# A hybrid decoder trunk on one core: two low parts of w_out by accumulating DMA, four sample readouts in one VectorE step each, the last samples and the last scan step moved up

## The chip, the cores and the metric

The kernel runs on one core of one Trainium2 chip. The metric is the device time of one execution in microseconds (us). A core has TensorE (PE; its weight loads are listed apart as PEld), VectorE (DVE), ScalarE (ACT), GpSimd (POOL) and SyncE (SP), which here only issues DMAs. Each works through its own list of instructions in a fixed order, and semaphores hold an instruction back until what it needs is there.

## What is computed

One step of a decoder layer for 512 new tokens of one prompt and one new token of each of 8 running sequences, 520 columns in all: a half-step SwiGLU FFN, a mixer, a second half-step FFN, a final norm, all in fp32. The mixer, cut to what matters:

```python
proj = h @ w_in                                   # u_pool, z, xbc, dt
pool_out = pooling mixer of u_pool                # 512 columns
xs, B, C = silu(causal_conv(xbc))
y, h_new = ssd_scan(xs, dt, A, B, C, state)       # chunks of 128 tokens, 2 groups of 8 heads
y = (y + d_skip * xs) * silu(z)
y = rms_norm per group (512 columns each) * ssd_norm
out = concatenate([pool_out, y]) @ w_out          # 1536 -> 1024
h = h + out
```

For a sample (one token of a running sequence) the scan is one step: the readout is the state's rows (128 per pair of heads) times C, summed over the 128 state columns, times the decay, plus a term from the new token.

## The kernel before

**Matmuls in three terms.** Every large product is made of fp32r matmuls of a high and a low part: `mm3` (lines 146, 149, 150) issues whi·xhi, whi·xlo and wlo·xhi into one PSUM bank. A weight unit is a tile of 128x1024 (512 KB). `load_unit` fetches it into one of four raw buffers with a DMA on SP's queue (L142); `split` has ScalarE cast it to whi (L134) and VectorE subtract to get wlo = raw - whi (L136). There are three homes for a pair of parts (thi/tlo, and two of whi/wlo), so a unit's cast waits until the matmuls of the unit before last but one are done. The FFNs have a second way, `part_by_dma` (L230): ScalarE makes the high part and then minus the high part, and a DMA of GpSimd's queue adds the weights from HBM to it.

**The mixer's order** is written by hand in three strings. `CONV_PLAN` does the inputs of the convolution and the first scan steps; `GATE_PLAN` the rest; `LAST_PLAN` joins the last units of w_out to the second FFN's start. A letter names a stage: z a unit of the gate's projection, p, c, m the pooling, A and B the two halves of a scan step (`ssd_a`, `ssd_b`; numbers 0 to 7 are four chunks of two groups), s that many samples, G the gate of one group (it needs all samples and scan steps of its group), H its norm, o, g, h the units of w_out for the pooled part and for groups 0 and 1 (`wout`), e small outputs. The order of the plan gives each instruction its rank. A scheduler at compile time then lays out each engine's list: by rank, among what its own model of the time holds ready. So VectorE's list interleaves stages, while TensorE's follows the plan nearly everywhere. Instructions under `keep_in_program_order` (the samples') stand behind all that their engine has from earlier in the plan.

**A sample** (`sample`, L1088): two loads on SP's queue, C's row for all partitions (L1090, two buffers) and the state of four head pairs (L1092, four buffers); VectorE multiplies them, 128x512 (L1094); ScalarE sums each quarter with four activations that accumulate into a column of `ysm` (L1097: an ACTIVATE and a read of the accumulator each).

**A scan step's second half** (`ssd_b`): TensorE makes yo, pst and yd in three PSUM banks; GpSimd scales the state hst (L1214), VectorE adds pst (L1215), combines yo and yd (L1218, L1219) and puts the result into X (L1222). In the mixer the PSUM pool has eight banks, taken in turn; a unit of w_out takes four, which L1243 adds to h.

**Gate and norm.** `gate` (G): scales ysm, adds it into X's sample columns (L1104, L1105, L1257), multiplies X by silu of z (L1254, L1259). `gate_out` (H): squares on ScalarE (L1265), adds on VectorE (L1268), a matmul with ones into psr_y (L195, plain fp32), root (L198) and reciprocal (L199), then the factor (L1276) and high and low part of the group's operand catg (L1277, L1278).

Of the kernel before, what the change touches and what calls it, by code (L numbers as in the profile page):

```python
# [13 lines left out]
ALU = mybir.AluOpType  # L14
# [21 lines left out]
LOW_ON_DVE = ((2, 0), (3, 0), (KF - 1, 1))  # L36
ON_ACT = 4
STATES = ((1, 1, 1, 1), (6, 17, 19, 20, 21), 4)
LOW_BY_DMA = {1: (2, 3, 4, 5, 6), 2: (*range(7), 9, 11)}

CONV_PLAN = (
    "b0 b1 d0 b2 b3 x0 x1 v0 d1 x2 x3 d2 X0 p0 y0 c0 A0 k0 p1 x4 m0 x5 B0 c1 p2 m1 A1 x6 c2 A2 B1 x7 X1 m2 A3"
)
GATE_PLAN = (
    "z0 B2 A4 z1 B3 p3 s1 z2 B4 s2 z3 c3 A5 s2 s2 z4 m3 B5 s2 A6 z5 e0 s2 G0 z6 A7 s2 z7 B6 s2 o0 H0 o1 B7 s1 G1 o2 "
    "o3 g0 g1 H1 g2 g3"
)
LAST_PLAN = "h0 h2 h1 n0 h3 n1 n2 n3"
# [15 lines left out]
def tile_trunk_step(ctx: ExitStack, tc: tile.TileContext, ins: dict, outs: dict):  # L64
# [165 lines left out]
    def part_by_dma(hi, lo, s, home):  # L230
        nc.scalar.copy(hi, s)
        nc.scalar.activation(out=lo, in_=hi.bitcast(F32), func=AF.Copy, scale=-1.0)
        nc.gpsimd.dma_start(out=lo, in_=home, accum_op=ALU.add)
# [22 lines left out]
    class Ffn:  # L256
# [175 lines left out]
        def quarter(self, f):  # L432
# [7 lines left out]
            if len(src.shape) == 3:  # L440
                h, l = (t.rearrange("p (j c) -> p j c", j=4) for t in (hi, lo))
            if f in LOW_BY_DMA[self.i] and (f, 1) not in LOW_ON_DVE:
                part_by_dma(h, l, src, self.dram[f][1][:, 512:])
# [90 lines left out]
        def stream(self, before, last_chunk):  # L534
# [6 lines left out]
            for t in tiles:  # L541
                for _ in range(STATES[0][t.d] if not isinstance(t, int) else t in STATES[1]):
                    next(self.states, None)
# [68 lines left out]
        def down_by_half(self, c, lo, after, wd):  # L612
            n = KF - lo
            banks, units = {}, []
            for d in range(KD):
                if d < STATES[2]:
                    next(self.states)
# [156 lines left out]

    ps[0] = tc.alloc_tile_pool(name="ppm", bufs=8, space=PSUM, reuse_waits="tile")
    mixer(tc, ins, outs, dict(locals()))
    f2["xg"].release()
    xa[0].release()
# [69 lines left out]
def mixer(tc, ins, outs, e):  # L848
    nc = tc.nc
    cst, act, wp, tmp, dr, pool = (e[x] for x in ("cst", "act", "wp", "tmp", "dr", "pool"))  # L850
    ones, queued, squared = e["ones"], e["queued"], tuple(e["added"])
    bank, load_unit, mm3, ws, v, rstd, rstds, vec, h, nx2, raw_tile, open_f2, fin, fill = (
        e[x] for x in ("bank", "load_unit", "mm3", "ws", "v", "rstd", "rstds", "vec", "h", "nx2", "raw_tile",
                       "open_f2", "fin", "fill"))
    xh, xl, _, r = nx2[0]
# [195 lines left out]
    ysm = mp.tile([P, NX, NS], F32, tag="ysm", name="ysm")  # L1051
# [4 lines left out]
    def rows_bc(b, a, g):  # L1056
        return scr_bc.rearrange("b (a g n) -> b a g n", a=2, g=2)[b, a, g].unsqueeze(0).to_broadcast([P, P])
# [27 lines left out]
        nc.vector.tensor_tensor(out=sxdt[:, gs], in0=sdt[:, gs], in1=X[:, gs, SEQ:NT], op=ALU.mult)  # L1085


    def sample(b, g):  # L1088
        cb = tmp.tile([P, HB], F32, tag="ta", name=f"cb{b}{g}")[:, :P]
        nc.sync.dma_start(out=cb, in_=rows_bc(b, 1, g))  # L1090
        h0 = mp.tile([P, 4, P], F32, tag="h0", bufs=4, name=f"h0_{b}{g}")
        nc.sync.dma_start(out=h0, in_=ins["state_ssm"][:, b, 4 * g : 4 * g + 4])  # L1092
        tc.keep_in_program_order(
            nc.vector.tensor_tensor(out=h0, in0=h0, in1=cb.unsqueeze(1).to_broadcast([P, 4, P]), op=ALU.mult))  # L1094
        for q in range(4):
            tc.keep_in_program_order(
                nc.scalar.activation(out=junk, in_=h0[:, q], func=AF.Copy,  # L1097
                                     accum_out=ysm[:, 4 * g + q, b : b + 1]))
# [53 lines left out]
    def ssd_a(c, g):  # L1152
        cs = slice(c * CH, (c + 1) * CH)
        pb = bank(f"pb{c}{g}")
        nc.tensor.transpose(pb[:, :P], BC[:, g, cs], ident)
        nc.tensor.matmul(pb[:, P : 2 * P], BC[:, g, cs], BC[:, 2 + g, cs], start=True, stop=True)
        bt = mp.tile([P, P], F32, tag="bt", bufs=3, name=f"bt{c}{g}")
        nc.scalar.copy(bt, pb[:, :P])
        scm = mp.tile([P, P], F32, tag="scm", bufs=3, name=f"scm{c}{g}")
        nc.vector.tensor_tensor(out=scm, in0=pb[:, P : 2 * P], in1=tri, op=ALU.mult)  # L1160
        px = bank(f"px{c}{g}")
        for q in range(4):
            nc.tensor.transpose(px[:, q * P : (q + 1) * P], X[:, 4 * g + q, cs], ident)
        ab = mp.tile([P, 8, P], F32, tag="ab", bufs=3, name=f"ab{c}{g}")
        nc.sync.dma_start(out=ab, in_=scr_acs[c * NH + 8 * g : c * NH + 8 * g + 8].unsqueeze(0).to_broadcast([P, 8, P]))
        dtc = tok[:, 0, c, 8 * g : 8 * g + 8]
        atc = tok[:, 1, c, 8 * g : 8 * g + 8]
        we = mp.tile([P, 8], F32, tag="we", bufs=2, name=f"we{c}{g}")
        nc.gpsimd.tensor_tensor(out=we, in0=ab[:, :, CH - 1], in1=atc, op=ALU.subtract)
        nc.scalar.activation(out=we, in_=we, func=AF.Exp)  # L1170
        E = cd = None
        if c > 0:
            E = mp.tile([P, 4, P], F32, tag="E", bufs=2, name=f"E{c}{g}")
            for j in range(2):
                nc.scalar.activation(out=E[64 * j : 64 * j + 64], in_=ab[64 * j : 64 * j + 64, j::2, :], func=AF.Exp)
            cd = mp.tile([P, 8], F32, tag="cd", bufs=2, name=f"cd{c}{g}")
            nc.scalar.activation(out=cd, in_=ab[:, :, CH - 1], func=AF.Exp)
        G = ab
        for q in range(ON_ACT):
            nc.scalar.activation(out=G[:, q], in_=ab[:, q], func=AF.Relu, scale=-1.0, bias=atc[:, q : q + 1])  # L1180
        for q in range(ON_ACT, 8):
            nc.vector.tensor_scalar(out=G[:, q], in0=ab[:, q], scalar1=atc[:, q : q + 1], scalar2=0.0,
                                    op0=ALU.subtract, op1=ALU.min)
        with queued(*(held["silu"] if (c, g) == (3, 0) else ())):
            nc.scalar.activation(out=G[:, :ON_ACT], in_=G[:, :ON_ACT], func=AF.Exp, scale=-1.0)
            held["exp"] = nc.scalar.activation(out=G[:, ON_ACT:], in_=G[:, ON_ACT:], func=AF.Exp)
        xdt = mp.tile([P, 8, 64], F32, tag="xdt", bufs=2, name=f"xdt{c}{g}")
        nc.vector.tensor_tensor(out=xdt, in0=px.rearrange("p (a b) -> p a b", a=8),
                                in1=dtc.unsqueeze(2).to_broadcast([P, 8, 64]), op=ALU.mult)
        xw = mp.tile([P, 8, 64], F32, tag="xw", bufs=2, name=f"xw{c}{g}")  # L1190
        nc.gpsimd.tensor_tensor(out=xw, in0=xdt, in1=we.unsqueeze(2).to_broadcast([P, 8, 64]), op=ALU.mult)
        with queued(*(held["catp"] if (c, g) == (0, 0) else ())):
            nc.vector.tensor_tensor(out=G, in0=G, in1=scm.unsqueeze(1).to_broadcast([P, 8, P]), op=ALU.mult)
        pair[c, g] = bt, xdt, xw, G, E, cd
# [35 lines left out]
            nc.vector.tensor_tensor(out=zbox[0][:, j, hs], in0=bs[b][:, :HB], in1=r[:, hs], op=ALU.mult)  # L1230

    def wout(cat, j, d2, fin=None):
        wh, wl = load_unit(ins["w_out"][j, d2], 1024, f"wo{j}{d2}", behind.get((j, d2), ()))
        for d in (2 * d2, 2 * d2 + 1):
            for b, hs in enumerate(HALVES):
                if d != 1 or j != 2:
                    ps = bank(f"wo{j}_{d}{b}")
                else:
                    ps = e["ps"][0].tile([P, 512], F32, tag="A", bufs=2, name=f"wo{j}_{d}{b}")
                for k in range(4):  # L1240
                    i = (d % 2) * 4 + k
                    mm3(ps[:, :HB], ws(wh, i), ws(wl, i), cat[:, 0, k, hs], cat[:, 1, k, hs], k == 0, k == 3)
                nc.vector.tensor_tensor(out=h[:, d, hs], in0=ps[:, :HB], in1=h[:, d, hs], op=ALU.add)  # L1243
                if fin is not None:
                    fin(d, b, hs)

    cats, behind = {}, {}
# [35 lines left out]

    smp = [(b, g) for g in range(2) for b in range(NS)]

    def samples(n):
        for _ in range(n):
            if smp:
                sample(*smp.pop(0))

    pooled, box = [], {}

    def ssd(c):
        return c % NC, c // NC

    def outs_a():
# [14 lines left out]
        "c": lambda j: pooled[j][0](),  # L1311
        "m": lambda j: pooled[j][1](),
        "s": samples,
        "A": lambda j: ssd_a(*ssd(j)),
        "B": lambda j: ssd_b(*ssd(j)),
        "z": zproj,
        "o": lambda j: wout(catp, 0, j),
        "G": gate,
        "H": gate_out,
        "g": lambda j: wout(cats[0], 1, j),  # L1320
        "h": lambda j: wout(cats[1], 2, j, fin),
        "n": fill,
        "e": lambda j: outs_a(),
# [101 lines left out]
```

## Time and profile before

| | |
|---|---|
| Median of 3 runs | 962.92 us (962.7 to 964.66) |
| The profiled execution | 963.72 us, its span 961.9 us |
| Instructions | 19663 |
| HBM read and written | 128.67 MB and 7.34 MB |
| POOL busy | 144.9 us (15%) |

The span runs from the first to the last instruction of the profiled execution. The profile lists busy time of each engine; a wait is put down to the engine, line and tile that came last, as "who <- for whom: total, times, longest"; the chain of waits follows the end of the program back through what released each step. In a row of the timeline the numbers are start and duration in us, and brackets hold the idle time before it and what ended it. In a row of a tile they are shortest, median and longest duration in ns, with the first and last start. A matmul is pipelined, so its duration is longer than its distance to the next.

### The profile page before, as it was taken

The page shows a single profiled execution, that of the slowest core. Times are in us where ns is not written, and L with a number is a line of the kernel's source. Part 1 is how long each engine was busy: PE and PEld are TensorE (multiplying, and loading weights), DVE is VectorE, ACT ScalarE, POOL GpSimd, SP SyncE. Part 2 cuts the span into 40 slices and gives each one's busy share as a digit, 9 for nine tenths or more (in the row PEclk, how much of TensorE's full clock was granted, in tenths as well). Part 3 has the DMA queues.
Part 4 walks back from the last instruction along what each step waited for, and adds up shares of the span by engine and source line. Part 5 has one row for each costly group of instructions (what it writes and reads, how often), then busy time and mean ns, then how long its engine had stood idle before and what let it go on. Part 6 is the DMA issues. An engine that isn't in the chain of part 4 may idle for free. (4 is left out here: it accounts for less than half of the span.)

```text
span 961.9 us, 19663 instructions
## 1 busy us (share of the span) xinstructions
PE 945.5 (98%) x7652; PEld 926.2 (96%) x7652; DVE 852.3 (89%) x1460; ACT 641.2 (67%) x1208; POOL 144.9 (15%) x228
## 2 busy tenths in 40 slices
PE   9999999999999999999999999999999999999996
PEld 8999999999999999999999999999999999999995
DVE  6999899998988788779979998898889999989886
ACT  7777756677566455485688645777776676766763
POOL 0011100001000001046252000112112101122120
PEclk9999999999999999999999999999999999999998
DMA  7665553455544243363355323457666646666642
GB/s 210 181 166 149 142 165 112 123 147 141 159 123 115 87 133 101 93 195 117 111 157 166 108 89 121 110 126 171 166 154 188 160 126 155 174 176 175 185 144 90
DMA packets 53629, 137.29 MB, mean 143 GB/s; under 512 B 7640, under 2 KB 15768, under 8 KB 53536
## 3 DMA queue, kind: packets, MB, share of 16 engines
q1 hardware_dynamic: 39840, 104.18, 33.6%
q0 software_dynamic: 13424, 31.73, 17.2%
q8 instruction: 60, 0.98, 0.4%
q14 instruction: 33, 0.27, 0.1%
q10 hardware_dynamic: 272, 0.13, 0.0%
HBM read 128.67 MB, written 7.34 MB: 141 GB/s over the span
## 5 line engine op out<-in xcount | busy, mean ns | idle before, releaser
L476 ACT COPY ac<-A 128x260 f32<-128x260 f32 x85 | 31.7, 373 | 34.7 <-PE A L150 33.5
L412 DVE TENSOR_TENSOR s<-raw 128x1024 f32<-128x1024 f32 x39 | 47.6, 1220 | 3.6 <-DMA raw<-in_w2gu 2.5
L476 ACT COPY ac<-BE 128x260 f32<-128x260 f32 x41 | 15.4, 376 | 30.0 <-PE BE L150 29.0
L146 PE MATMUL inx<-xh_mx,whi_inx 128*128 128x260 f32 x112 | 31.8, 284 | 0.0
L149 PE MATMUL inx<-xl_mx,whi_inx 128*128 128x260 f32 x112 | 31.6, 282 | 0.0
L150 PE MATMUL inx<-xh_mx,wlo_inx 128*128 128x260 f32 x112 | 31.6, 282 | 0.0
L977 DVE SCALAR_TENSOR_TENSOR A<-U,h,A 128x544 f32<-128x544 f32 x36 | 28.8, 799 | 1.1 <-ACT A L975 0.7
L295 PE MATMUL P<-x,raw 128*128 128x260 f32 x128 | 28.9, 387 | 0.0
L295 PEld LDWEIGHTS P<-x,raw 128*128 128x128 f32 x128 | 24.6, 193 | 4.0 <-DMA raw<-in_w1gu 0.3
L146 PE MATMUL wo<-catg,whi_wo 128*128 128x260 f32 x96 | 27.6, 287 | 0.0
L134 ACT CAST thi<-raw 128x1024 fp32r<-128x1024 f32 (+1 forms) x14 | 14.2, 1012 | 20.0 <-PE wo L149 9.9
L150 PE MATMUL wo<-catg,wlo_wo 128*128 128x260 f32 x96 | 27.2, 283 | 0.0
L149 PE MATMUL wo<-catg,whi_wo 128*128 128x260 f32 x96 | 27.1, 282 | 0.0
L1097 ACT ACTIVATE junk<-h 128x128 f32<-128x128 f32 x64 | 19.7, 308 | 7.9 <-DVE h L1094 6.5
L150 PE MATMUL A<-xth_f,qs 128*128 128x260 f32 x84 | 24.0, 286 | 0.9 <-DMA qs<-in_w2gu 0.8
L1139 ACT ACTIVATE so<-br,sxdt 128x128 f32<-128x128 f32 x64 | 22.5, 375 | 3.3 <-DVE room L1141 3.1
L146 PE MATMUL A<-xth_f,qs 128*128 128x260 f32 x84 | 23.9, 284 | 0.0
L149 PE MATMUL A<-xtl_f,qs 128*128 128x260 f32 x84 | 23.7, 282 | 0.0
L237 DVE TENSOR_TENSOR gs<-gq,gs 128x780 fp32r<-128x780 f32 (+1 forms) x28 | 23.2, 829 | 0.4 <-ACT gs L236 0.4
L146 PE MATMUL inz<-xh_mx,whi_inz 128*128 128x260 f32 x80 | 22.9, 287 | 0.0
L149 PE MATMUL inz<-xl_mx,whi_inz 128*128 128x260 f32 x80 | 22.7, 284 | 0.0
L150 PE MATMUL inz<-xh_mx,wlo_inz 128*128 128x260 f32 x80 | 22.6, 283 | 0.0
(2530 smaller groups left out, 4747.3 us busy)
## 6 DMA issues: line engine op xcount, KB each, us to landing
raw<-in_w2gu SPq DMA_DIRECT2D x44, 512.0 KB, 4.2
raw<-in_w1gu SPq DMA_DIRECT2D x41, 512.0 KB, 4.1
raw<-in_w_in SPq DMA_DIRECT2D x24, 512.0 KB, 3.6
raw<-in_w1d SPq DMA_DIRECT2D x16, 512.0 KB, 4.3
raw<-in_w2d SPq DMA_DIRECT2D x16, 512.0 KB, 4.6
raw<-in_w_out SPq DMA_DIRECT2D x12, 512.0 KB, 3.6
ab<-scr_acs SPq DMA_DIRECT2D x8, 512.0 KB, 4.5
h<-in_state_ssm SPq DMA_DIRECT2D x16, 256.0 KB, 3.5
```

Of the source, the lines that this page charges most:

```text
L134: cast = nc.scalar.copy(h, src)
L146: first = nc.tensor.matmul(ps, whi, xhi, start=start, stop=False, **kw)
L149: nc.tensor.matmul(ps, whi, xlo, start=False, stop=False, **kw)
L150: nc.tensor.matmul(ps, wlo, xhi, start=False, stop=stop, **kw)
L237: low = nc.vector.tensor_tensor(out=lo, in0=s, in1=hi.bitcast(F32), op=ALU.subtract)
L295: mm = nc.tensor.matmul(self.banks[f, u][b][:, :HB], ws(self.raw[f][:, u], j + 4 * q), xg[:, slot[q]], start=j == q == 0, stop=j == 3 and ...
L412: nc.vector.tensor_tensor(out=s1, in0=diag, in1=up0, op=ALU.add)
L476: self.copied = nc.scalar.copy(keep, out[:, :HB]).ins
L977: nc.vector.scalar_tensor_tensor(out=A[:, :n], in0=U[:, j : j + n], scalar=w(j), in1=A[:, :n], op0=ALU.mult, op1=ALU.add)
L1097: nc.scalar.activation(out=junk, in_=h0[:, q], func=AF.Copy, accum_out=ysm[:, 4 * g + q, b : b + 1]))
L1139: nc.scalar.activation(out=o[:, q], in_=br, func=AF.Copy, scale=sxdt[:, j, b : b + 1]))
```

## The change

Three edits, all in the mixer's second half.

- `wout` takes the low part of units (1,0) and (1,1), which are g0 and g1, by `part_by_dma`.
- `sample` gets a flag: then VectorE sums all four quarters with one `tensor_reduce` of 128x4x128 into 128x4 instead of ScalarE's four activations. The letter r in the plan sets it.
- In `GATE_PLAN`, s1 and s2 at the front become r2 and r2; the last s1 goes, so each later sample comes one place sooner; B7 moves from behind o1 to in front of it.

```diff
+OUT_LOW_BY_DMA = ((1, 0), (1, 1))
...
 GATE_PLAN = (
-    "z0 B2 A4 z1 B3 p3 s1 z2 B4 s2 z3 c3 A5 s2 s2 z4 m3 B5 s2 A6 z5 e0 s2 G0 z6 A7 s2 z7 B6 s2 o0 H0 o1 B7 s1 G1 o2 "
+    "z0 B2 A4 z1 B3 p3 r2 z2 B4 r2 z3 c3 A5 s2 s2 z4 m3 B5 s2 A6 z5 e0 s2 G0 z6 A7 s2 z7 B6 s2 o0 H0 B7 o1 G1 o2 "
     "o3 g0 g1 H1 g2 g3"
 )
...
-    def sample(b, g):
+    def sample(b, g, reduce):
...
+        if reduce:
+            tc.keep_in_program_order(
+                nc.vector.tensor_reduce(out=ysm[:, 4 * g : 4 * g + 4, b], in_=h0, axis=mybir.AxisListType.X, op=ALU.add))
+            return
         for q in range(4):
...
     def wout(cat, j, d2, fin=None):
-        wh, wl = load_unit(ins["w_out"][j, d2], 1024, f"wo{j}{d2}", behind.get((j, d2), ()))
+        src, name = ins["w_out"][j, d2], f"wo{j}{d2}"
+        if (j, d2) in OUT_LOW_BY_DMA:
+            raw = raw_tile(name)
+            nc.sync.dma_start(out=raw, in_=src)
+            wh, wl = e["weight_homes"](1024, name, wp, 3, ("whi", "wlo"))
+            e["part_by_dma"](wh, wl, raw, src)
+        else:
+            wh, wl = load_unit(src, 1024, name, behind.get((j, d2), ()))
...
-    def samples(n):
+    def samples(n, reduce=False):
         for _ in range(n):
-            if smp:
-                sample(*smp.pop(0))
+            sample(*smp.pop(0), reduce)
...
+        "r": lambda n: samples(n, True),
```

`part_by_dma`, which the mixer did not call before:

```python
    def part_by_dma(hi, lo, s, home):
        nc.scalar.copy(hi, s)
        nc.scalar.activation(out=lo, in_=hi.bitcast(F32), func=AF.Copy, scale=-1.0)
        nc.gpsimd.dma_start(out=lo, in_=home, accum_op=ALU.add)
```

## The prediction, made before the changed kernel was run

> **What bounds the kernel now.** I read the busy line of the page first, then the waits of TensorE, then busy time by stretch around the mixer's second half, then the chain of waits there.
>
> ```profile
> PE 945.5 (98%) x7652; PEld 926.2 (96%) x7652; DVE 852.3 (89%) x1460; ACT 641.2 (67%) x1208; POOL 144.9 (15%) x228
> ```
>
> TensorE is busy for 945.5 of a span of 961.9 us: the whole kernel has about 16 us in which it could be faster without fewer matmuls, and the change takes no matmul away. So the question is which idle time of TensorE lies where the change works. The waits of TensorE by line (who, for whom, total us, times, longest):
>
> ```profile
> PE psr_y L195 <- DVE X L1268: 1.5, 1, 1.5
> PE A_Down(c=0, d=1)_8807 L150 <- DMA wlo_Down(c=0, d=1)a<-in_w2d: 1.4, 1, 1.4
> ```
>
> The longest wait of all, 1.5 us in one piece, is the gate's sum of squares (psr_y) waiting for VectorE's additions on L1268. The next one shows another thing that this change buys: a low part that comes by an accumulating DMA can arrive late, there in the second FFN. Stretch by stretch (us, busy time of each engine with instruction counts, clock, DMA share, GB/s):
>
> ```profile
> core 0: us, PE busy (x) PEld busy (x) DVE busy (x) ACT busy (x) POOL busy (x), PEclk, DMA share, GB/s
> 480.00:505.00 25.00, 24.92 (x213) 22.82 (x211) 17.87 (x38) 20.02 (x55) 12.27 (x11) 1.00 0.55 163
> 505.00:540.00 35.00, 35.00 (x287) 33.48 (x287) 34.73 (x65) 30.15 (x105) 5.30 (x4) 1.00 0.48 152
> 540.00:566.00 26.00, 24.60 (x209) 23.93 (x208) 25.96 (x53) 12.88 (x29) 0.68 (x1) 1.00 0.35 109
> ```
>
> TensorE runs at full clock with almost no gap until the stall, 1.5 us ahead of psr_y at 566.05; a matmul of 260 columns starts every 0.12 us (287 in 35.00). VectorE has 7.1 us free before 505 and then 0.3 us in the next 61: its queue is the limit that shows itself at the end of the stretch. ScalarE is nearly full up to 540 and half idle after it. The chain of waits into the stall (start us, us, what):
>
> ```profile
> 558.25 0.64 DVE X L1257 x4
> 558.96 0.46 issue
> 559.42 0.42 DVE h L1243
> 559.84 1.83 DVE zs L1259 x3
> 561.67 0.34 DVE h L1243
> 562.01 1.13 DVE wlo_wo L136
> 563.14 0.67 DVE h L1243 x2
> 563.81 1.15 DVE X L1268
> 564.96 0.34 DVE h L1243
> 565.30 0.62 DVE X L1268
> 565.92 0.14 issue
> 566.05 1.11 PE psr_y L195 x4
> ```
>
> What stands in front of this is the sixteenth sample: its product (the last L1094, whose row is below) starts at 554.2, because its step stands behind scan step B7 in the plan; ScalarE sums it until 556.7, gate G1 adds it in (L1257), multiplies (L1259), has ScalarE square, and adds (L1268); VectorE does its steps between other units' evacuations and low parts.
>
> **The change part by part.** First the low parts of units g0 and g1 (w_out 1,0 and 1,1), two of the five wlo_wo subtractions of this stretch, with B7's three VectorE steps between them:
>
> ```profile
> 545.04 0.68 DVE L1218 TENSOR_TENSOR E<-yo,E 128x512 f32<-128x512 f32 x1
> 545.64 1.22 DVE L136 TENSOR_TENSOR wlo_wo<-raw,whi_wo 128x1024 fp32r<-128x1024 f32 x1
> 546.77 0.68 DVE L1215 TENSOR_TENSOR hst<-pst,hst 128x512 f32<-128x512 f32 x1
> ...
> 549.72 0.68 DVE L1219 TENSOR_TENSOR E<-yd,E 128x512 f32<-128x512 f32 x1
> ...
> 551.99 1.22 DVE L136 TENSOR_TENSOR wlo_wo<-raw,whi_wo 128x1024 fp32r<-128x1024 f32 x1
> ```
>
> Each holds VectorE for 1.13 us to the next start, so 2.3 us leave the full stretch. In their place ScalarE negates the high part and GpSimd adds the weights to it by DMA:
>
> ```profile
> L381 ACT ACTIVATE wlo_Down(c=0, d=0)a<-whi_Down(c=0, d=0)a x2: 1061/1062/1062, 96.4 to 688.6; 128x1024 fp32r<-128x1024 f32 x2
> ```
>
> ```profile
> DMA to landing us min/median/max: 3.5/5.0/8.3
> ```
>
> ```profile
> 541.41 1.03 ACT L134 CAST whi_wo<-raw 128x1024 fp32r<-128x1024 f32 x1
> 543.33 2.60 ACT L1277 ACTIVATE catg<-zs,h 128x520 fp32r<-128x520 f32 x4 [0.88 <-DVE zs L1276]
> 547.25 1.05 ACT L134 CAST whi_wo<-raw 128x1024 fp32r<-128x1024 f32 x1 [1.33 <-PE wo L149]
> ```
>
> ```profile
> L146 PE MATMUL wo<-catg,whi_wo x96: 277/282/473, 552.9 to 610.7; 128*128 128x260 f32 x96
> ```
>
> The second row is of all the kernel's accumulating DMAs on L382, from issue to landing. Unit g0: cast at 541.41 to 542.44, negation 1.06, so the DMA can go at 543.5 and lands at 548.5 (median) to 551.8 (longest); TensorE opens g0 at 552.9 and needs the low part one matmul pair later. Unit g1: cast 547.25, DMA at 549.4, landing 554.4 to 557.7, wanted a unit (48 matmuls, 5.8 us) after g0, at 558.7. Both fit, g0 with 1 us to spare at the longest, and GpSimd has no other work there but B7's product (0.68 us busy in 26). The 2.1 us on ScalarE lie in its idle half. Behind the waiting GpSimd DMAs nothing is queued until the second FFN, and on SP's queue the later w_out loads gain: their raw buffer is free after the cast, without the subtraction. So this part costs nothing while those margins hold. The Trainium skill's page "DMA: Bandwidth & Descriptors", section "Anatomy of one DMA — SWDGE (gpsimd) path", fits such a DMA as 2.0 us plus its bytes over 436 GB/s; by that estimate these 512 KB would land after 3.2 us, g0 would have over 5 us to spare, and the rival of a late low part would fall away. The landings above are longer and decide.
>
> Second, four samples are summed by VectorE:
>
> ```profile
> L1097 ACT ACTIVATE junk<-h x64: 291/310/314, 485.6 to 556.3; 128x128 f32<-128x128 f32 x64
> L1097 ACT ACTIVATION_READ_ACCUMULATOR junk<-h x64: 185/187/197, 485.8 to 556.5; 128x1 f32 x64
> ```
>
> ```profile
> L1094 DVE TENSOR_TENSOR h<-h,cb x16: 675/680/1022, 483.2 to 554.2; 128x512 f32<-128x512 f32 x16
> ```
>
> ```profile
> 537.98 3.42 DVE L199 RECIPROCAL yr<-yr 128x260 f32<-128x260 f32 x2 [0.20 <-ACT yr L198]
> ```
>
> ScalarE loses 16 pairs of 0.31 and 0.19, 8.0 us, of which some 7 show, since neighbours overlap. VectorE gains four reductions of 128x512. No reduction is in this trace. Lower end: 0.60 each, the pace of a 512-wide product; upper end: the reciprocal's 1.71 us for 260 columns, scaled to 512, 3.4 each. I take 0.7 (2.8 us in all), since a sum reads one operand once as the product reads two. They sit with the first two pairs of samples, from 483 on, in the 7.1 us that VectorE has free before 505; part of that was spent waiting for ScalarE, which now has less to do. So: nothing. At the upper end 13.6 us would overrun the gap by 6.5. The Trainium skill's page "VectorE: DVE Perf Modes", section "Rules for kernel authors", calls the reduction VectorE's slowest op and advises against it on a hot path; if that meant the upper end it would undo the whole change, but its perf-mode table gives it the plain one-element rate, as the product has, and the sum by it is the same.
>
> Third, samples start one earlier everywhere (r2 for s1), so the sixteenth goes with the last pair, behind B6, which is this one today:
>
> ```profile
> 534.69 1.28 DVE L1094 TENSOR_TENSOR h<-h,cb 128x512 f32<-128x512 f32 x2
> ```
>
> That is near 535 instead of 554. Its loads are issued on SP's queue one place sooner too; four of these buffers are now freed by VectorE rather than by a queued ScalarE, so SP waits less for them.
>
> Fourth, B7 stands before o1. TensorE does the same matmuls, but psr_y of H0 (plain fp32) is now followed by plain fp32 scan work, and one change of mode goes:
>
> ```profile
> 532.51 0.47 PE L146 MATMUL wo<-catp,whi_wo 128*128 128x260 f32 x1
> ```
>
> ```profile
> 541.32 0.39 PE L146 MATMUL wo<-catp,whi_wo 128*128 128x260 f32 x1
> ```
>
> These first matmuls of o1 (behind psr_y) and o2 (behind B7) take 0.47 and 0.39 against a median of 0.28. In the new order only the one behind B7 is left: 0.19 us.
>
> **Sum.** G1's inputs, sample sixteen and B7's X, come some 10 us sooner, and the queue in front of L1268 is 2.3 us shorter; either alone exceeds the 1.5 us stall, so it goes: -1.5. The switch: -0.2. What is late next on TensorE is the catg1 chain for h0, which now also starts earlier, so nothing. Together -1.7. The profiled execution took 963.72 us (span 961.9), 0.8 above the median of 962.92; on it the sum gives 962.0, on the median **961.2**, which I predict.
>
> **Rivals.** (1) *Low part late.* If the order on ScalarE puts g0's negation behind the four catg copies (ending 545.9), it ends at 547.0 and lands at 552.0 to 555.3: a wait of up to 2.3 us takes the place of the one removed, 961.2 to 963.5. For it: the 1.4 us wait on exactly such a DMA in the second FFN. Against: ScalarE is idle for 0.88 us just there, and the median fits even so.
>
> (2) *Slower: the scan's PSUM banks.* The mixer takes eight banks in turn. With B7 before o1, the last three banks of o2 are those that B7's yo, pst and yd held, where now o3 gets them. They come free when VectorE reads them, today at 545.7, 547.4 and 550.4, because the reciprocals and the gate's products go first. In the new order o2 opens near 541.2 again (B7 and o1 only change places) and wants them 12, 24 and 36 matmuls later, at 542.6, 544.1 and 545.5. If VectorE's order keeps B7's reads where they are, TensorE stands 4.9 us, less the 1.7: **966.1**. It decides from the point where L1219 ends later than 547.2, and is slower by 0.2% only when it ends after 549.1. Against: B7's outputs are there 6 us sooner and its reads now rank before o1's and o3's work, so they should run near 537, before the reciprocals.
>
> (3) *Nothing gained.* VectorE stays full to 566 because other units' work fills what was freed, or L1268 keeps its place behind it: 962.9.
>
> (4) *More gained.* The shifted order also spares the second FFN its late low part (1.4 us): 959.8.
>
> **Chances.** What a measurement of this kernel can tell from no change is about 0.2%, 1.9 us. Forecast (a gain of 1.0 to 2.4) 0.54, of which 0.26 is beyond 1.9; rival 1 0.12 and rival 3 0.09, all within; rival 4 0.10, faster; rival 2, with a reduction at its upper end (0.02), 0.15, all slower. So faster 0.36, same 0.49, slower 0.15. The range reaches from rival 4 (959.8, with no more below than 0.04) up past rivals 1 and 3 to a third of rival 2: 959.8 to 964.2. The forecast's own range is 960.5 to 961.9.
>
> **What would show it.** Right: no wait of psr_y on L1268 and the last L1094 near 535; the four banks of o2 without a gap; no TensorE wait on wlo_wo; reductions near 0.7 us; 48 of ScalarE's L1097 pairs instead of 64; three wlo_wo subtractions instead of five up to 566. Wrong: a wait of TensorE on L1219 or on a wlo_wo DMA, VectorE full before 505, or stalls elsewhere in place of this one. The prediction is wrong as a whole if TensorE's idle time outside 480 to 620 moves by more than a microsecond, since nothing here argues about that.

## The result and the profile after

| | before | after |
|---|---|---|
| Median of 22 runs each | 962.7 us (959.27 to 964.92) | 960.8 us (958.51 to 963.76) |
| Ratio of after to before | | 0.9982, 95% interval 0.9974 to 0.9990 |
| The profiled execution, its span | 963.72, 961.9 us | 962.74, 961.0 us |

The change gains 1.7 us by the ratio (0.0018 of 962.7), with an interval of 1.0 to 2.5. The profiled execution of after lies 1.9 above its median, so its span says less than the stretch in which the change works. The lines of the changed file stand further down: L1268 is now L1280, L1094 is L1095, L1097 is L1102, L195 is L196, L136 is L137; the reduction is L1098, the negation L233 and its DMA L234.

Busy time of the engines, and TensorE's waits by line, in the kernel after:

```profile
PE 945.7 (98%) x7652; PEld 926.8 (96%) x7652; DVE 852.9 (89%) x1462; ACT 637.5 (66%) x1178; POOL 148.4 (15%) x230
```

```profile
PE A L151 <- DMA qs<-in_w2gu: 1.5, 2, 1.1
PE px L1168 <- ACT X L980: 1.2, 1, 1.2
...
PE A_Down(c=0, d=2)_8930 L151 <- DMA wlo_Down(c=0, d=2)a<-in_w2d: 0.6, 1, 0.6
```

The 1.5 us wait of psr_y is gone. What is left stands elsewhere: in the FFNs, and at 467 us (px, transposes in a scan step's first half), ahead of the changed stretch. There the two profiles differ by about a microsecond in each direction, and so do those of the experiments (e4, the same kernel up to there, has no wait of px): that is the scatter of the runs, not the change. In all, TensorE is idle outside 480 to 620 for 14.8 us before and for 15.1 after, so the prediction's last sign of being wrong, more than a microsecond there, did not come.

Busy time by stretch, after:

```profile
480.00:505.00 25.00, 25.00 (x214) 23.14 (x213) 20.64 (x43) 16.01 (x33) 13.93 (x11) 1.00 0.61 176
505.00:540.00 35.00, 34.89 (x292) 32.68 (x290) 35.00 (x66) 29.36 (x101) 5.98 (x4) 1.00 0.44 135
540.00:566.00 26.00, 26.00 (x216) 25.87 (x215) 24.50 (x51) 13.62 (x27) 1.76 (x2) 1.00 0.62 162
```

TensorE is now busy for 26.00 of the 26 us in which it stood 1.4 before. VectorE took 2.8 us more up to 505 (20.64 for 17.87), is as full as can be up to 540, and has 1.5 us free after that. TensorE's busy time from 480 to 620 as one row, before and then after:

```profile
480.00:620.00 140.00, 138.37 (x1093) 131.66 (x1092) 124.93 (x227) 95.44 (x234) 23.28 (x21) 1.00 0.44 130
```

```profile
480.00:620.00 140.00, 139.79 (x1105) 133.11 (x1104) 126.89 (x231) 92.13 (x205) 26.64 (x23) 1.00 0.49 139
```

1.4 us of idle time are gone (1.63 to 0.21). The change of mode that is saved, from plain fp32 matmuls to fp32r ones (0.2), lies in busy time and comes on top. Together that is 1.6 of the measured 1.7.

VectorE around B7 and at the end of the stretch, after (start, duration, then engine, line, operation):

```profile
536.12 1.28 DVE L1095 TENSOR_TENSOR h<-h,cb 128x512 f32<-128x512 f32 x2
...
539.13 1.77 DVE L200 RECIPROCAL yr<-yr 128x260 f32<-128x260 f32 x1
540.81 0.62 DVE L1223 TENSOR_TENSOR E<-yo,E 128x512 f32<-128x512 f32 x1
541.36 1.76 DVE L200 RECIPROCAL yr<-yr 128x260 f32<-128x260 f32 x1
543.04 0.62 DVE L1220 TENSOR_TENSOR hst<-pst,hst 128x512 f32<-128x512 f32 x1
...
543.68 0.68 DVE L1224 TENSOR_TENSOR E<-yd,E 128x512 f32<-128x512 f32 x1
...
560.87 0.68 DVE L1280 TENSOR_TENSOR X<-X 128x520 f32<-128x520 f32 x1
```

```profile
565.43 1.04 PE L196 MATMUL psr_y<-X,ones 128*128 128x260 f32 x4
```

The last product of the samples runs at 536 instead of 554. L1280 ends at 561.55, and TensorE takes psr_y at 565.43 in its own turn: 3.9 us to spare where 1.5 were missing.

### The profile page after: what moved, and what is told of

Read it like the earlier page. It is cut to its first block, busy times and chain, and to the rows that moved or that the text cites. A ratio compares the mean times of both kernels' runs of the same rounds, so it can differ in the third digit from the quotient of the medians.

```text
span 961.0 us, 19637 instructions
## 1 busy us (share of the span) xinstructions
PE 945.7 (98%) x7652; PEld 926.8 (96%) x7652; DVE 852.9 (89%) x1462; ACT 637.5 (66%) x1178; POOL 148.4 (15%) x230
## 4 chain that ended last, share of the span: by engine, by line
PE 83%; DVE 5%; DMA 5%; issue 3%; ACT 2%; POOL 1%; DVEq 0%; SPq 0%; POOLq 0%; ACTq 0%
PE A L151 8%; PE A L147 8%; PE A L150 8%; PE BE L150 6%; PE BE L147 6%; PE BE L151 6%; PE P L296 4%; PE wo L147 2%; PE wo L151 2%; PE wo L150 2%; DMA qs<-in_w2gu 2%; PE inz L147 1%; PE inz L151 1%; PE inz L150 1%; PE dh L151 1%
## 5 line engine op out<-in xcount | busy, mean ns | idle before, releaser
L1255 DVE TENSOR_TENSOR h<-wo,h 128x260 f32<-128x260 f32 x48 | 19.0, 418 | 4.8 <-PE wo L151 4.8
```

## The experiments

All times are ratios to the kernel before, timed beside it on the same chip, with 95% intervals. An effect of 1.5 us is 0.0016, and half an interval is about 0.0013, so each run is read by its waits first and by its time second.

| Run | what it is | TensorE's wait of psr_y | ratio |
|---|---|---|---|
| e1 | both low parts by DMA alone | none | 0.9981 [0.9968, 0.9993] |
| e2 | reductions alone | 1.4 | 0.9997 [0.9984, 1.0011] |
| e3 | order alone | 0.3, and 1.4 of inz | 1.0014 [0.9999, 1.0029] |
| e4 | after, B7 back behind o1 | none | 0.9977 [0.9966, 0.9988] |
| e5 | after, all samples reduced | 5.8, and 2.6 of wo | 1.0097 [1.0080, 1.0114] |
| e6 | after without the DMAs | 0.2 | 0.9980 [0.9968, 0.9993] |
| e8 | low part of g1 alone by DMA | 1.2 | 0.9989 [0.9978, 1.0000] |
| e9 | both low parts by DMA, B7 ahead of o1 | none, but 0.7 of wo | 0.9994 [0.9983, 1.0006] |
| e10 | low part of g0 alone by DMA | none | 0.9975 [0.9962, 0.9988] |
| e11 | sixteenth sample alone reduced | 2.2 | 1.0008 [0.9991, 1.0024] |

### One part at a time: e1, e2, e3

e1 is before's plan with the new `wout`:

```diff
-    "z0 B2 A4 z1 B3 p3 r2 z2 B4 r2 z3 ... s2 o0 H0 B7 o1 G1 o2 "
+    "z0 B2 A4 z1 B3 p3 s1 z2 B4 s2 z3 ... s2 o0 H0 o1 B7 s1 G1 o2 "
```

> Only the low parts of units g0 and g1 by accumulating DMA; the order of the plan and ScalarE's sums as before. Theory (the stall ahead of psr_y is VectorE's full queue, so 2.3 us taken out of it are enough): the wait of psr_y on the last additions to X is under 0.3 us, the time 1.2 to 1.5 us below before, ratio 0.9984 to 0.9988. Rival (the stall hangs on the sixteenth sample's start behind B7, whatever the queue holds): the wait stays above 1 us, ratio 1.000. Rival (low part late): a wait of TensorE on wlo_wo of 0.5 to 2.3 us in place of it, ratio 0.9995 to 1.001.

e2 has before's order and low parts, with r for s at the front:

```diff
-OUT_LOW_BY_DMA = ((1, 0), (1, 1))
+OUT_LOW_BY_DMA = ()
-    "z0 B2 A4 z1 B3 p3 r2 z2 B4 r2 z3 ... s2 o0 H0 B7 o1 G1 o2 "
+    "z0 B2 A4 z1 B3 p3 r1 z2 B4 r2 z3 ... s2 o0 H0 o1 B7 s1 G1 o2 "
```

> Only the sums of the first three samples by VectorE, in the old places; no low part by DMA. Theory (the reductions only fill room of VectorE before 505 us and ScalarE is no bound): the wait of psr_y stays 1.3 to 1.7 us, ratio 0.9995 to 1.0005. Rival (ScalarE, 6 us lighter, is what lets the end of the half come sooner): the wait falls under 0.7 us, ratio 0.9985 to 0.9992.

e3 has the new order, with all sums on ScalarE and all low parts on VectorE:

```diff
-OUT_LOW_BY_DMA = ((1, 0), (1, 1))
+OUT_LOW_BY_DMA = ()
-    "z0 B2 A4 z1 B3 p3 r2 z2 B4 r2 z3 ... s2 o0 H0 B7 o1 G1 o2 "
+    "z0 B2 A4 z1 B3 p3 s2 z2 B4 s2 z3 ... s2 o0 H0 B7 o1 G1 o2 "
```

> Only the order: samples one earlier, B7 ahead of o1; all sums by ScalarE and all low parts by VectorE as before. Theory (the sixteenth sample and B7's X some 10 us sooner are enough by themselves): no wait of psr_y above 0.3 us and one change of mode of TensorE saved, 1.5 to 1.7 us below before, ratio 0.9982 to 0.9984. Rival (VectorE's queue decides and nothing leaves it): the wait stays near 1.5 us, only the 0.2 us of the mode are gained, ratio 0.9998. Rival (ScalarE, with one sample more at the front, becomes late there): TensorE waits for ScalarE before 505 us, ratio 1.000 or above.

In e1 the last additions on VectorE, with the row behind them, and psr_y on TensorE are:

```profile
560.07 0.70 DVE L1280 TENSOR_TENSOR X<-X 128x520 f32<-128x520 f32 x1
560.67 1.22 DVE L137 TENSOR_TENSOR wlo_wo<-raw,whi_wo 128x1024 fp32r<-128x1024 f32 x1
```

```profile
563.05 1.04 PE L196 MATMUL psr_y<-X,ones 128*128 128x260 f32 x4
```

The additions end 2.3 us ahead of need, so the theory holds: the low parts alone are enough, and e1 gains as much as the whole change, as far as the times can tell. e2's wait is the old one, so the reductions by themselves gain nothing, as the theory said. e3's waits of TensorE:

```profile
PE inz L147 <- DVE zs L1235: 1.4, 1, 1.4
...
PE psr_y L196 <- DVE X L1280: 0.3, 1, 0.3
```

Its theory falls, and its third case is what came, one step removed: TensorE waits for VectorE, which ScalarE has made late at the front. The wait can be followed back. First ScalarE, then VectorE, then TensorE, in e3:

```profile
488.04 1.03 ACT L135 CAST thi<-raw 128x1024 fp32r<-128x1024 f32 x1
```

```profile
489.10 2.17 DVE L137 TENSOR_TENSOR tlo<-raw,thi 128x1024 fp32r<-128x1024 f32 x1 [2.60 <-ACT thi L135]
...
504.71 0.69 DVE L1095 TENSOR_TENSOR h<-h,cb 128x512 f32<-128x512 f32 x1 [2.47 <-DMA cb<-scr_bc]
505.32 0.42 DVE L1235 TENSOR_TENSOR zs<-inz,r_mx 128x260 f32<-128x260 f32 x1
```

```profile
505.79 0.39 PE L147 MATMUL inz<-xh_mx,thi 128*128 128x260 f32 x1 [1.36 <-DVE zs L1235]
```

The same subtraction in the kernel before:

```profile
488.23 1.79 DVE L136 TENSOR_TENSOR tlo<-raw,thi 128x1024 fp32r<-128x1024 f32 x1 [1.09 <-ACT thi L134]
```

Two samples at the front mean eight sums on ScalarE instead of four, and the cast of thi stands behind them in ScalarE's list. VectorE waits 2.6 us for that cast, 1.5 more than the 1.1 in the kernel before; the lateness goes on to the samples at 500, so the next row of C is asked for later, and VectorE stands at 502 waiting for it with L1235 behind (in the kernel before this wait is as long, but ends 0.8 us earlier). L1235 reads the PSUM bank that TensorE wants. In the kernel before the same read comes just in time: it ends at 504.91, and TensorE goes on at 504.97. So order alone trades one stall for another.

### Order with reductions, without the DMAs: e6

```diff
-OUT_LOW_BY_DMA = ((1, 0), (1, 1))
+OUT_LOW_BY_DMA = ()
```

> The order and the four reductions of the kernel after, but both low parts subtracted by VectorE as before. Theory (in e3 the second sample's sums on ScalarE made the cast of thi 1.7 us late, and that lateness reached TensorE as the wait of inz; the reductions take it away, and the sixteenth sample's early start does the rest): no wait of inz above 0.4 us, psr_y waits under 0.4 us, ratio 0.9982 to 0.9988. Rival (the low parts alone are the gain; without them the queue is full whatever stands first in it): psr_y waits 0.5 to 1.5 us, ratio 0.9992 to 1.000.

TensorE's wait:

```profile
PE psr_y L196 <- DVE X L1280: 0.2, 1, 0.2
```

The theory holds: with the reductions in it the front has no wait of inz, and 0.2 is left of the stall. This also tests the chain followed back in e3, since only the reductions differ. Order and reductions together do nearly what the low parts do alone; the change does it twice over.

### The length of VectorE's queue: e8, e10, e11, e5

e8 and e10 are e1 with one unit each; e11 is the kernel before with r1 for the last s1; e5 is the kernel after with r2 for every s2:

```diff
-OUT_LOW_BY_DMA = ((1, 0), (1, 1))
+OUT_LOW_BY_DMA = ((1, 1),)
```

```diff
-OUT_LOW_BY_DMA = ((1, 0), (1, 1))
+OUT_LOW_BY_DMA = ((1, 0),)
```

```diff
-... o0 H0 o1 B7 s1 G1 o2
+... o0 H0 o1 B7 r1 G1 o2
```

```diff
-... c3 A5 s2 s2 z4 m3 B5 s2 A6 z5 e0 s2 G0 z6 A7 s2 z7 B6 s2 ...
+... c3 A5 r2 r2 z4 m3 B5 r2 A6 z5 e0 r2 G0 z6 A7 r2 z7 B6 r2 ...
```

> The kernel before with one low part by accumulating DMA, that of unit g1 alone; the order and ScalarE's sums as before. Theory (the stall is the length of VectorE's queue, 1.13 us of it a subtraction): psr_y still waits, 0.2 to 0.6 us, ratio 0.9986 to 0.9992. Rival (the gain is a step, by which unit is spared): the wait is 1.3 us or more, or none.

> The kernel before with one low part by accumulating DMA, that of unit g0 alone. Theory (from the run with g1 alone: the 1.13 us that leave VectorE's queue are mostly lost again where it waits for ScalarE's cast of thi, which then stands behind the sixteenth sample's sums): a wait of VectorE for thi of 0.7 to 1.1 us near 555 us, psr_y still waits 1.0 to 1.4 us, ratio 0.9993 to 0.9999. Rival (g0's place, ahead of the catg copies, is the one that counts): psr_y waits under 0.5 us, ratio 0.9985 to 0.999.

> The kernel before with the sixteenth sample alone summed by VectorE, in its old place behind B7. Theory (VectorE's queue sets the stall): 0.68 us are added to it, psr_y waits 1.9 to 2.4 us, ratio 1.0004 to 1.001. Rival (the chain from the sixteenth sample through ScalarE's four sums sets it): 2 us of ScalarE leave that chain, psr_y waits 0 to 0.8 us, ratio 0.9984 to 0.9993.

> The kernel after, with all sixteen samples summed by VectorE instead of four. Theory (VectorE's queue is the limit from 505 us on): twelve reductions of 0.68 us, 8.2 us, come into a stretch without room; less the 3.5 us that psr_y's inputs are early in the kernel after, TensorE waits some 4 to 5 us for VectorE, in one place or several, ratio to before 1.002 to 1.004. Rival (ScalarE's sums hold the samples' buffers and loads, so its relief shortens the half): no wait of TensorE above 0.5 us, ratio 0.998 or below.

e11 bears the theory out to the tenth: one reduction more, and the wait is longer by its length.

```profile
556.07 0.68 DVE L1098 TENSOR_REDUCE ysm<-h 128x4 f32<-128x512 f32 x1
```

```profile
PE psr_y L196 <- DVE X L1280: 2.2, 1, 2.2
```

Its rival falls: the sixteenth sample's four sums on ScalarE are not what the stall hung on. e8 should then have left 0.4 and left 1.2. ScalarE and VectorE there:

```profile
552.53 0.31 ACT L1102 ACTIVATE junk<-h 128x128 f32<-128x128 f32 x1 [4.21 <-DVE h L1095]
...
553.71 1.03 ACT L135 CAST thi<-raw 128x1024 fp32r<-128x1024 f32 x1
```

```profile
554.77 1.23 DVE L137 TENSOR_TENSOR tlo<-raw,thi 128x1024 fp32r<-128x1024 f32 x1 [0.94 <-ACT thi L135]
...
556.91 0.64 DVE L1269 SCALAR_TENSOR_TENSOR X<-X,h,ysm 128x8 f32<-128x8 f32 x4
```

VectorE's list reaches the sixteenth sample's product more than 1 us sooner, three of its sums now stand ahead of the cast of thi on ScalarE, where before all four stood behind it, and VectorE, which has tlo next, waits 0.94 for the cast. Of 1.13 us freed, 0.2 to 0.3 are left. From this I expected the same of e10, and was wrong. The same stretch of e10:

```profile
551.83 1.21 DVE L137 TENSOR_TENSOR wlo_wo<-raw,whi_wo 128x1024 fp32r<-128x1024 f32 x1
...
554.62 0.64 DVE L1269 SCALAR_TENSOR_TENSOR X<-X,h,ysm 128x8 f32<-128x8 f32 x4
555.18 0.69 DVE L1271 TENSOR_TENSOR zs<-X,zs 128x520 f32<-128x520 f32 x1
555.79 1.22 DVE L137 TENSOR_TENSOR tlo<-raw,thi 128x1024 fp32r<-128x1024 f32 x1
...
563.06 0.68 DVE L1280 TENSOR_TENSOR X<-X 128x520 f32<-128x520 f32 x1
```

```profile
563.89 1.11 PE L196 MATMUL psr_y<-X,ones 128*128 128x260 f32 x4
```

Here the list that the compiler laid out has the gate's L1269 and the first L1271 ahead of tlo, and not behind it as before and in e8; and g1's own subtraction (551.83) stands behind the sixteenth sample's product (550.89), where before it stood ahead. So all four sums and the cast of thi (553.22 to 554.25) run while VectorE has other work; it waits for nothing, and one evacuation (0.34) less stands ahead of L1280. Which of the two moved places decides, the runs do not separate. L1280 ends at 563.74, 0.15 ahead of psr_y. That is the distance at which a psr_y that waits is released (0.14 in the kernel before), so e10 is just in time, with nothing to spare. One unit of 1.13 us is thus worth 0.3 or all of the 1.5, by what the new list puts around it. In e1 three subtractions fewer stand ahead of L1280 and not two: that of the next unit (560.67 above; 561.92 before, ahead of both L1268) now stands behind it. That is most of why its inputs come 3.8 us sooner than before for 2.3 us taken out; three evacuations fewer are about the rest.

e5 has 8.2 us of reductions in a full stretch. Its waits of TensorE, and three short stretches behind the first of them:

```profile
PE psr_y L196 <- DVE X L1280: 5.8, 1, 5.8
PE wo L147 <- DVE h L1255: 2.6, 1, 2.6
```

```profile
536.50:538.40 1.90, 1.83 (x4) 1.51 (x5) 1.90 (x4) 0.48 (x1) 0.00 (x0) 0.50 0.05 13
538.40:541.00 2.60, 2.60 (x11) 2.04 (x9) 2.60 (x6) 0.48 (x1) 0.51 (x1) 0.50 0.59 197
541.00:544.00 3.00, 3.00 (x26) 1.84 (x25) 3.00 (x4) 0.00 (x0) 0.53 (x1) 0.83 0.01 4
```

The direction is the theory's, the size is twice it. VectorE was full already at H0, the first gate's norm, which I had not counted: the spare 3.9 us belong to the second. At H0 the kernel after has 2.3 us to spare (L1280 ends at 530.41, psr_y starts at 532.67), and nine of the twelve reductions, with other work that the new list puts there, stand ahead of it. And after 5.8 us without work TensorE's granted clock is 0.50 in the two rows up to 541; the 0.83 of the next 3 us puts its return to 1.00 at about 542. The same psr_y, yo and pst take 5.4 us here (536.57 to 541.99) and 2.7 in the kernel after (532.67 to 535.39). Waits of 8.4 and 2.7 of slow clock, less the 1.5 and the 0.2 that the kernel after saves, make 9.4; measured are 9.3 (0.0097 of 962.3).

The Trainium skill's page "TensorE: Matmul & The Clock Gate", section "What's actually happening", says that the clock falls to half after an idle window of about 3.4 us and comes back after a busy one. The runs agree as far as they go, though none shows the length of the window: 0.50 after 5.8 us idle, back after some 5.4 us of work, and 1.00 in the row behind e11's wait of 2.2:

```profile
567.00:571.00 4.00, 4.00 (x32) 3.88 (x32) 2.97 (x2) 0.92 (x2) 0.00 (x0) 1.00 0.00 0
```

### The place of B7: e4 and e9

e4 is the kernel after with "o0 H0 o1 B7 G1 o2"; e9 is e1 with "o0 H0 B7 o1 s1 G1 o2".

> The kernel after with B7 back behind o1. Theory (sample sixteen's early start and the low parts' DMA each suffice; B7's place is worth only the mode change): no wait of psr_y above 0.3 us, first matmuls of o1 0.47 and of o2 0.39 us again, 0.2 us above the kernel after, ratio to before 0.9984. Rival (B7's early X is what removes the stall): a wait of psr_y of 0.5 to 1.5 us comes back, ratio 0.9989 to 1.000.

> Both low parts by accumulating DMA, and B7 ahead of o1; the samples and their sums as before. Theory (B7's place is worth one change of mode, 0.19 us, and nothing waits for it): no wait of TensorE above 0.3 us from 480 to 620 us, the first matmul of o1 0.47 us and that of o2 0.28 (one long one instead of two), ratio 0.9975 to 0.9982. Rival (with the sixteenth sample still behind o1, VectorE's order changes and B7's banks or X come late): a wait of 0.5 us or more of o2, of psr_y or of inz, ratio 0.999 or above.

e4 has no wait of TensorE from 480 to 620 us and is as fast as the kernel after (0.9977 and 0.9982, intervals over each other): the early X of B7 is not needed. The 0.2 of the mode are there in the profile and too small for the times. First matmuls of o1 and o2 in e4, then that of o1 in the kernel after:

```profile
532.51 0.47 PE L147 MATMUL wo<-catp,whi_wo 128*128 128x260 f32 x1
...
541.33 0.39 PE L147 MATMUL wo<-catp,whi_wo 128*128 128x260 f32 x1
```

```profile
536.42 0.39 PE L147 MATMUL wo<-catp,whi_wo 128*128 128x260 f32 x1
```

In e9 the rival came true, in a place of its own, and the theory's first matmul of o1 is 0.39 us, not 0.47, since B7 stands ahead of it as in the kernel after. TensorE's wait, and ScalarE:

```profile
PE wo L147 <- ACT yr L199: 0.7, 1, 0.7
```

```profile
537.12 0.48 ACT L199 ACTIVATE yr<-psr_y,eps 128x260 f32<-128x260 f32 x1
```

TensorE starts on the second bank of o1 at 537.65, when the L199 shown (it reads psr_y) has ended; the first matmul behind this wait takes 0.39 us too, so a long first matmul is not by itself a sign of a change of mode. In the kernel after, L199 runs later still (538.6) and no bank of o1 waits for it. Why the banks fall otherwise in e9 the rows do not say; that stays open.

## Why the prediction was right, and where not

**The stall and its size.** Forecast were -1.5 for the wait of psr_y and -0.2 for the mode, 961.2. Measured are -1.7 by the ratio and 960.8 as the median, and no wait of TensorE is listed from 480 to 620. That the size fits so well is in part a cap: a stall of 1.5 us gives no more than 1.5, so that the reliefs together are far larger (3.9 us to spare) does not show in the time.

**"Either alone exceeds the 1.5 us stall."** Right for the low parts (e1: no wait). For the order it failed twice: with the reductions 0.2 is left (e6), without them 0.3 is left and 1.4 appears at 505 (e3). What was wrong is to take an earlier start of the inputs for an equally earlier end of the additions: in e6 the last product of the samples starts near 535 instead of at 554, yet TensorE's wait for L1280 is only 1.3 us shorter, and VectorE is full up to there (24.00 of 24 us busy from 540 to 564). And the sum of 2.3 us for two low parts was too plain a count: VectorE's list is laid out anew, so that one of them gains 0.3 (e8), the other everything (e10), and both take a third subtraction out of the way (e1).

**The reductions at nothing.** Their duration was right:

```profile
L1098 DVE TENSOR_REDUCE ysm<-h x4: 673/675/693, 484.8 to 496.2; 128x4 f32<-128x512 f32 x4
```

0.68 us where 0.7 was taken, near the lower end of the range, and they lie in the room before 505 as foretold. But "nothing" was not the whole of it: they keep the second sample's sums out of ScalarE's way, without which the new order cost 1.4 us in e3. I had not priced the front without them.

**The low part of g0: the margin failed, not the result.** I gave it 1 us to spare at the longest landing, if ScalarE negates right behind the cast. ScalarE in the kernel after, then the DMA, its landing, and TensorE's first use:

```profile
542.36 1.05 ACT L232 CAST whi_wo<-raw 128x1024 fp32r<-128x1024 f32 x1
545.67 1.35 ACT L1289 ACTIVATE catg<-zs,h 128x520 fp32r<-128x520 f32 x2 [2.26 <-DVE zs L1288]
546.93 1.04 ACT L233 ACTIVATE wlo_wo<-whi_wo 128x1024 fp32r<-128x1024 f32 x1
```

```profile
548.27 0.90 POOL L234 DMA_DIRECT2D wlo_wo<-in_w_out  x1 [12.49 <-ACT wlo_wo L233]
```

```profile
DMA to landing us min/median/max: 5.7/6.4/7.1
```

```profile
554.04 0.39 PE L151 MATMUL wo<-catg,wlo_wo 128*128 128x260 f32 x1
```

The negation stands behind two of the four catg copies, 4.6 us after the cast began: half of the first rival, which has it behind all four. The DMA is issued at 548.27. Of the two landings only the shorter, 5.7, can be g0's: it gives 553.97, and TensorE takes the low part at 554.04. That first use lost 0.1 us; a landing as long as g1's 7.1 would have cost 1.4. So it was luck that this part cost no more. In e4 and e1 the DMA has time, since the negation follows the cast at once; from e4 the kernel after differs only in B7's place.

**The PSUM banks.** The slower rival asked whether VectorE reads yd by 547.2 with B7 ahead. It does, at 544.4: yo's read stands between the two reciprocals, those of pst and yd (543.04 and 543.68) behind both, but ahead of the gate's products (L1288, from 544.95). That is neither ahead of the reciprocals, near 537, as I wrote, nor where the rival needs it. No wait of o2 is listed, so that mechanism fell there; e9 shows its kind at o1. And in the rows of the kernel before, B7's first read (L1218) stands ahead of both subtractions and not between them, which changes nothing in the sum.

**The rest.** "Nothing gained" falls by e1 and e6. "More gained" is not shown: the late low part of 1.4 us is 0.6 in the waits above, but it is not listed at all in e2, which has neither the order nor the DMAs, so its size is scatter; and TensorE's idle time from 620 on hardly moves (12.9 us before, 12.7 after).

## What to carry to other kernels

When one full queue makes a stall, several small reliefs may each be enough: try them singly, since here one constant with one entry (e10) does as much as the whole change, as far as the times can tell, though with nothing to spare where the whole change has 3.9 us. Time taken out of an in-order queue counts only if what stands next in it is ready; look for the instruction that the freed engine reaches early, and for what that one waits on. An earlier step brings its whole train to every engine it touches, and the wait it makes may show up 15 us later on another engine.

## What the runs showed of the hardware

The accumulating DMA of 512 KB landed after 5.7 to 7.1 us here, where those of the FFNs had a median of 5.0; with the two low parts as the only change in e1 it was the same:

```profile
DMA to landing us min/median/max: 5.9/6.9/8.0
```

The estimate that the prediction gave from the Trainium skill's page "DMA: Bandwidth & Descriptors", section "Anatomy of one DMA — SWDGE (gpsimd) path", 3.2 us, is half of that; why these take longer, no run here separates. And a stall of 5.8 us costs TensorE 2.7 us more through its clock, while the 2.6 us wait of the same run left it at 1.00 from 566 to 620.
